# Band attention in fixed rounds, keys a tile ahead, the softmax division on GpSimd

## The chip, the cores and the metric

The kernel runs on one core of a Trainium2 chip. The metric is device time in microseconds (us) of one execution, as the median of several runs. The core has five engines with queues of their own: TensorE (PE in the profile, its weight loads PEld), VectorE (DVE), ScalarE (ACT), GpSimd (POOL) and SyncE (SP), which issues the DMAs here.

## The reference

The reference is one inference step of a one-layer hybrid encoder, width 1024, over 2048 prompt frames and eight running streams of 16 new frames each. One input projection feeds three mixers (band attention, a gated delta rule, a diagonal state-space model); their outputs are concatenated, projected, normed, and pass through a feed-forward block. The change concerns the attention alone: eight heads of width 64, in which a frame sees its own 64-frame chunk and the eight before it, with a learned bias by distance.

```python
s = einsum('bqhd,bkhd->bhqk', qc, kc) * scale + bias
s = where(valid, s, NEG_INF)
p = softmax(s, axis=-1)
return einsum('bhqk,bkhd->bqhd', p, vc)
```

The streams do the same with 512 cached keys and values and their 16 new ones.

## The kernel before

The program has three stages: the projection with the two other mixers, the attention, and then output projection and feed-forward. The change lies in the attention (`attention`, L1071 to L1293).

The prompt is cut into 16 tiles of 128 frames, the heads into four pairs. A tile sees at most five key tiles (its own and four before), fewer in tiles 0 to 3. For each tile and pair:

- `a_scores` multiplies queries by keys. Queries and keys are split into a high part and a rest, stacked on the partitions, so that two matmuls (L1184, L1185) give each segment of scores at full precision; a head has one segment per key block of 512 frames, at most two. VectorE adds the bias and keeps the running extreme (L1186), ScalarE takes the exponential with its sum (L1189), VectorE the reciprocal (L1191) and then the product with it, in place (L1194).
- `a_values` transposes the weights block by block on TensorE (L1212), copies them from PSUM alternately on ScalarE (L1215) and VectorE (L1217), and multiplies by the values (L1220). After the fourth pair the tile's output is copied (L1223) and stored.

`a_kblock` splits the keys of four tiles at once (L1133, L1134), `a_tile` the queries of one (L1155 to L1157). `a_sample` handles one stream whole: its loads, scores (L1269), division (L1274), transposes (L1278, L1282), values (L1289, L1290) and copy (L1293). Streams run in tiles 1 to 8, `w_part` splits a piece of the output projection's weights in tiles 2 to 9.

The values of a pair are written down two pairs behind its scores (`AHEAD` = 2). That order is only the order of writing: the framework's scheduler decides how each engine's instructions are queued, TensorE's too. It allocates a tile's buffer when one of its tag is free, and sets the semaphores.

Of the kernel before, what the change touches and what calls it, by code (L numbers as in the profile page):

```python
# [19 lines left out]
SEQ = 2048  # L20
# [10 lines left out]
AHEAD = 2  # L31
# [13 lines left out]
class K:  # L45
# [1025 lines left out]
    def attention(self, es):  # L1071
# [17 lines left out]
        self.kst, self.vt = {}, {}  # L1089
# [6 lines left out]
        todo = []  # L1096
        for i in range(16):
            t = self.a_tile(i)
            for p in range(4):
                todo.append((t, p, self.a_scores(t, p)))  # L1100
                if len(todo) > AHEAD:
                    self.a_values(*todo.pop(0))
            if 2 <= i <= 9:
                self.w_part(i - 2)
            if 1 <= i <= 8:
                self.a_sample(i - 1)
                if i == 8:
                    nc.sync.dma_start(self.mixT[0:512, SEQ:NT].rearrange("(f p) t -> p f t", p=128), self.sos)

        w0 = c.tile([128, 5, 8, 128], F32, name="w0", tag="nb")  # L1110
        for x in todo:
            self.a_values(*x)
# [4 lines left out]

    def tsplit(self, parts, t):
        src, sl = self.at_a(parts, t)
        return src[:, sl].rearrange("(f p) t -> p f t", p=128)  # L1120

    def a_kblock(self, b):

        nc = self.nc
        ks = self.ak.tile([128, 8, 512], F32R, name="kst", tag="kst")
        for i in range(4):
            kr = self.ak.tile([128, 4, 128], F32, name="kr", tag="kr", bufs=2)
            nc.sync.dma_start(kr, self.tsplit(self.kT, b * 4 + i))
            ts = slice(i * 128, (i + 1) * 128)
            for q in range(2):  # L1130
                r, o = slice(q * 64, q * 64 + 64), slice(64 - q * 64, 128 - q * 64)
                hi = ks[r, q::2, ts]
                nc.scalar.copy(hi, kr[r])  # L1133
                nc.vector.tensor_tensor(ks[o, q::2, ts], kr[r], hi.bitcast(F32), OP.subtract)  # L1134
        self.kst[b] = ks

    def a_tile(self, i):
# [3 lines left out]
        aw = self.aw  # L1141
        b, r = divmod(i, 4)
        if r == 0:
            self.a_kblock(b)
        v = aw.tile([128, 512], F32, name="vt", tag="vt", bufs=6)
        vsrc, sl = self.at_a(self.vS, i)
        nc.sync.dma_start(v, vsrc[sl])
        self.vt[i] = v
        qr = aw.tile([128, 4, 128], F32, name="qr", tag="qr", bufs=2)
        nc.sync.dma_start(qr, self.tsplit(self.qT, i))  # L1150
        qd = aw.tile([128, 8, 128], F32R, name="qd", tag="qd")
# [7 lines left out]
        return dict(i=i, qd=qd, ql=ql, vt=[self.vt[j] for j in range(j0, i + 1)], kst=dict(self.kst), ob=None)  # L1159

    def a_scores(self, t, p):

        nc = self.nc
        V, mm = nc.vector, nc.tensor.matmul
        aw = self.aw
        i, qd, ql, kst = t["i"], t["qd"], t["ql"], t["kst"]
# [6 lines left out]
        for q in range(2):  # L1173
# [4 lines left out]
            if n1:  # L1178
                segs.append((kst[b - 1], min(512 - 128 * n1, 320), 512, 512 - 128 * n1, 0, 128 * n1))
            segs.append((kst[b], 0, max(128 * n2, 192), 0, 128 * n1, 128 * n2))  # L1180
            low = 3e38
            for ks, c0, c1, d0, x0, n in segs:
                ps = self.asp.tile([128, 512], F32, name="aps", tag="s")
                mm(ps[:, c0:c1], qd[:, h], ks[:, h, c0:c1], start=True, stop=False)  # L1184
                mm(ps[:, c0:c1], ql[:, h], ks[:, h, c0:c1], start=False, stop=True)  # L1185
# [11 lines left out]
    def a_values(self, t, p, P):  # L1197
# [28 lines left out]
    def sample_setup(self, es):  # L1226
# [10 lines left out]
        for q in self.sQ:  # L1237
            nc.gpsimd.memset(q, 0.0)
# [547 lines left out]
```

## Time and profile before

| | |
|---|---|
| median of 3 runs | 2952.27 us (2949.34 to 2952.82) |
| the profiled execution's own time | 2949.45 us |
| its span, first to last instruction | 2947.7 us |
| mean granted clock of TensorE | 0.981 of full speed |
| busy: TensorE, VectorE, ScalarE, GpSimd | 2803.6, 1996.0, 1324.7, 930.5 us |

Busy is the time in which an engine had an instruction in it. Matmuls overlap in the array and their ends are modelled, so TensorE's busy time does not say that it ran at its peak. The granted clock is a share of 2.4 GHz; 0.50 is 1.2 GHz.

### The profile page before, as it was taken

Reading aid. Unit: us, or ns where it says so; the run is one execution under the profiler, and the core shown is the slowest. Engines: PE = TensorE matmul, PEld = TensorE weight load, DVE = VectorE, ACT = ScalarE, POOL = GpSimd, SP = SyncE. Lnnn points to the kernel's source line nnn. Section 1 sums busy time; section 2 is a strip of 40 time slices with the busy share of each in tenths; the row PEclk is TensorE's granted clock in tenths of the full one; section 3 lists DMA queues with packets and bytes.
Section 4 is the critical chain, followed back from the end, with each engine's and each line's share of the span. In section 5 each row is a group of like instructions: output and inputs, shape, how many; then the busy total and the mean of one; then the engine's idle time right before and its main releaser. Section 6 shows DMA issues by size and latency. Waiting matters only on the chain.

```text
span 2947.7 us, 46191 instructions
## 1 busy us (share of the span) xinstructions
PE 2803.6 (95%) x16677; PEld 2451.0 (83%) x16677; DVE 1996.0 (68%) x5093; ACT 1324.7 (45%) x2735; POOL 930.5 (32%) x842
## 2 busy tenths in 40 slices
PE   8999999989999999999999999988999998899996
PEld 8988888867777777788889899967999897799996
DVE  7588887797655778778755555497555557855557
ACT  3554544342456666612334344453334345444442
POOL 0011111231100000002554544554544445555653
PEclk9999999989999999999999999999999999999998
DMA  5634454464557441144512122133112122422221
GB/s 183 199 106 127 108 138 112 131 174 122 179 195 224 141 129 51 58 168 165 185 66 86 57 67 77 58 118 122 61 63 81 58 72 95 144 76 73 86 86 43
DMA packets 282923, 330.37 MB, mean 112 GB/s; under 512 B 84530, under 2 KB 217478, under 8 KB 282374
## 3 DMA queue, kind: packets, MB, share of 16 engines
q1 hardware_dynamic: 282694, 327.42, 35.5%
q8 instruction: 131, 2.15, 0.3%
q14 instruction: 98, 0.80, 0.1%
HBM read 265.04 MB, written 64.93 MB: 112 GB/s over the span
## 4 chain that ended last, share of the span: by engine, by line
PE 71%; DVE 15%; DMA 4%; ACT 3%; issue 3%; POOL 3%; SPq 0%; ACTq 0%; POOLq 0%; DVEq 0%
PE fdp L68 7%; PE fdp L69 7%; PE fdp L70 7%; PE pps L69 3%; PE pps L70 3%; PE pps L68 3%; PE aob L1220 2%; PE fupx L69 2%; PE fupx L68 2%; PE fupx L70 2%; PE wops L69 2%; PE wops L68 2%; PE wops L70 2%; PE fupz L70 2%; PE fupz L68 2%
## 5 line engine op out<-in xcount | busy, mean ns | idle before, releaser
L1459 POOL TENSOR_TENSOR wu<-wur,wu 128x512 fp32r<-128x512 f32 x329 | 444.5, 1356 | 683.1 <-ACT wu L1458 672.7
L1585 DVE TENSOR_TENSOR fy<-fy,fdp 128x512 f32<-128x512 f32 x500 | 342.3, 687 | 306.2 <-PE fdp L70 306.0
L68 PE MATMUL fdp<-wdh,hh 128*128 128x512 f32 x1068 | 419.8, 395 | 21.6 <-DVE fy L1583 12.2
L70 PE MATMUL fdp<-wdh,hl 128*128 128x512 f32 x1068 | 418.1, 392 | 1.1 <-DVE hl L1520 1.1
L69 PE MATMUL fdp<-wdl,hh 128*128 128x512 f32 x1068 | 418.7, 392 | 0.0
L1458 ACT CAST wu<-wur 128x512 fp32r<-128x512 f32 x329 | 202.9, 619 | 421.3 <-DMA wur<-in_w_upL 165.1
L68 PE MATMUL pps<-xh,wh 128*128 128x384 f32 (+2 forms) x800 | 280.5, 352 | 9.0 <-ACT xh L63 8.6
L69 PE MATMUL pps<-xl,wh 128*128 128x384 f32 (+2 forms) x800 | 279.5, 350 | 2.9 <-DVE xl L64 2.8
L70 PE MATMUL pps<-xh,wl 128*128 128x384 f32 (+2 forms) x800 | 277.5, 347 | 0.5 <-DVE wl L64 0.3
L68 PEld LDWEIGHTS fdp<-wdh,hh 128*128 128x128 f32 x1068 | 202.2, 190 | 66.0 <-DVE fy L1583 13.8
L70 PEld LDWEIGHTS fdp<-wdh,hl 128*128 128x128 f32 x1068 | 202.1, 189 | 44.3 <-DVE hl L1520 1.9
L69 PEld LDWEIGHTS fdp<-wdl,hh 128*128 128x128 f32 x1068 | 202.1, 189 | 40.2
L63 ACT CAST wdh<-wdr 128x1024 fp32r<-128x1024 f32 x94 | 98.1, 1049 | 262.9 <-PE fdp L70 262.9
L1520 DVE TENSOR_TENSOR hl<-fre,hh 128x384 fp32r<-128x384 f32 (+1 forms) x186 | 137.7, 743 | 71.5 <-ACT hh L1519 71.5
L68 PEld LDWEIGHTS pps<-xh,wh 128*128 128x128 f32 x800 | 152.2, 191 | 19.7 <-ACT xh L63 9.1
L69 PEld LDWEIGHTS pps<-xl,wh 128*128 128x128 f32 x800 | 152.2, 190 | 14.3 <-DVE xl L64 5.4
L70 PEld LDWEIGHTS pps<-xh,wl 128*128 128x128 f32 x800 | 151.9, 190 | 11.3 <-issue 1.8
L64 DVE TENSOR_TENSOR wl<-wr,wh 128x512 fp32r<-128x512 f32 (+1 forms) x152 | 105.3, 699 | 61.1 <-ACT wh L63 57.9
L63 ACT CAST wh<-wr 128x512 fp32r<-128x512 f32 (+1 forms) x152 | 92.8, 619 | 78.2 <-DMA wr<-in_w_inA 39.7
L64 DVE TENSOR_TENSOR wdl<-wdr,wdh 128x1024 fp32r<-128x1024 f32 x94 | 116.1, 1237 | 3.1 <-ACT wdh L63 3.1
L1427 POOL TENSOR_TENSOR fxc<-fxs 128x256 f32<-128x256 f32 x17 | 20.8, 1223 | 294.8 <-ACT fxs L1417 288.8
L1189 ACT ACTIVATE P<-P,st 128x640 f32<-128x640 f32 (+4 forms) x128 | 97.2, 761 | 35.5 <-DVE st L1186 35.3
(555 smaller groups left out, 7289.9 us busy)
## 6 DMA issues: line engine op xcount, KB each, us to landing
wur<-in_w_upL SPq DMA_DIRECT2D x96, 512.0 KB
wdr<-in_w_dnL SPq DMA_DIRECT2D x96, 512.0 KB
wr<-in_w_inA SPq DMA_DIRECT2D x70, 512.0 KB
TU<-tD SPq DMA_DIRECT2D x34, 256.0 KB
y<-in_x SPq DMA_DIRECT2D x17, 512.0 KB
x<-y SPq DMA_DIRECT2D x17, 512.0 KB
fxr<-x SPq DMA_DIRECT2D x17, 512.0 KB
fy<-x SPq DMA_DIRECT2D x17, 512.0 KB
```

What stands on the lines that cost most here:

```text
L63: nc.scalar.copy(hi, src)
L64: nc.vector.tensor_tensor(lo, src, hi.bitcast(F32), OP.subtract)
L68: mm(out, lh, rh, start=first, stop=False, **kw)
L69: mm(out, lh, rl, start=False, stop=False, **kw)
L70: mm(out, ll, rh, start=False, stop=last, **kw)
L1189: nc.scalar.activation(x, x, AF.Exp, scale=-1.0, bias=st[:, q:q + 1], accum_out=st[:, 2 + q:3 + q])
L1220: mm(ob[q * 64:q * 64 + 64, p], vt[j][:, h * 64:(h + 1) * 64], PT[:, k], start=j == 0, stop=j == nk - 1)
L1427: P.tensor_tensor(c1, b["B12"], b["B11"], OP.subtract)
L1458: self.nc.scalar.copy(hi, src)
L1459: P.tensor_tensor(lo, src, hi.bitcast(F32), OP.subtract)
L1520: V.tensor_tensor(hl, r, hh.bitcast(F32), OP.subtract)
L1585: V.tensor_tensor(y[:, zs], y[:, zs], ps, OP.add)
```

## The change

The order of the attention's matmuls on TensorE is written by hand and kept: `mm` and `turn` ask the framework to hold them in program order, from the second round on. A round is one pair of one tile. It issues the scores of its pair, the values of the pair two rounds back, and the transposes of the pair one round back (`a_values` is split into `a_turn` and `a_values`). The product with the reciprocal moves from VectorE to GpSimd (`a_norm`), for the streams too.

The keys are no longer split four tiles at once: `a_load` and `a_keys` load and split those of the next tile during the third round of this one, into two fixed buffers, of which one stretch is filled with zeros at the start. A stream's work is spread over a tile's rounds: scores in the first, transposes in the second, values in the third, and the next stream's K and V are loaded after the scores and the values.

```diff
+        self.kst = [c.tile([128, 8, 512], F32R, name=f"kst{i}") for i in range(2)]
+        for k in self.kst:
+            nc.gpsimd.memset(k[:, :, 128:192].bitcast(F32), 0.0)
...
-        for i in range(16):
-            t = self.a_tile(i)
-            for p in range(4):
-                todo.append((t, p, self.a_scores(t, p)))
-                if len(todo) > AHEAD:
-                    self.a_values(*todo.pop(0))
-            if 2 <= i <= 9:
-                self.w_part(i - 2)
-            if 1 <= i <= 8:
-                self.a_sample(i - 1)
...
+                if streams and p == 0:
+                    sample = self.s_scores(b)
+                    if b < 7:
+                        self.s_load_k(b + 1)
+                if streams and p == 2:
+                    self.s_values(b, sample)
+                    if b < 7:
+                        self.s_load_v(b + 1)
+                rounds.append(self.a_scores(t, p))
+                if len(rounds) > 2:
+                    self.a_values(rounds.pop(0))
+                if len(rounds) > 1:
+                    self.a_turn(rounds[0])
+                self.a_norm(rounds[-1])
+                self.pinned = True
+                if streams and p == 1:
+                    self.s_turn(sample)
+                if i < 15:
+                    if p == 1:
+                        self.a_load(i + 1)
+                    elif p == 2:
+                        self.a_keys(i + 1)
+                    elif p == 3:
+                        t1 = self.a_tile(i + 1)
+                if p == 3 and 2 <= i <= 9:
+                    self.w_part(i - 2)
...
+    def mm(self, *a, **kw):
+
+        i = self.nc.tensor.matmul(*a, **kw)
+        if self.pinned:
+            self.tc.keep_in_program_order(i)
...
+    def a_load(self, i):
+        nc = self.nc
+        kr = self.ak.tile([128, 4, 128], F32, name="kr", tag="kr", bufs=2)
+        nc.sync.dma_start(kr, self.tsplit(self.kT, i))
+        qr = self.aw.tile([128, 4, 128], F32, name="qr", tag="qr", bufs=2)
+        nc.sync.dma_start(qr, self.tsplit(self.qT, i))
+        self.ld_[i] = kr, qr
+
+    def a_keys(self, i):
+
+        nc = self.nc
+        kr, ks = self.ld_[i][0], self.kst[i // 4 % 2]
+        ts = slice(i % 4 * 128, i % 4 * 128 + 128)
+        for q in range(2):
+            r, o = slice(q * 64, q * 64 + 64), slice(64 - q * 64, 128 - q * 64)
+            hi = ks[r, q::2, ts]
+            nc.scalar.copy(hi, kr[r])
+            nc.vector.tensor_tensor(ks[o, q::2, ts], kr[r], hi.bitcast(F32), OP.subtract)
+        v = self.aw.tile([128, 512], F32, name="vt", tag="vt", bufs=6)
         vsrc, sl = self.at_a(self.vS, i)
         nc.sync.dma_start(v, vsrc[sl])
         self.vt[i] = v
...
-        rs = aw.tile([128, 2], F32, name="rs", tag="ars", bufs=4)
-        V.reciprocal(rs, st[:, 2:4])
+        return dict(t=t, p=p, P=P, st=st, nk=nk)
+
+    def a_norm(self, s):
+        P, st = s["P"], s["st"]
+        rs = self.aw.tile([128, 2], F32, name="rs", tag="ars", bufs=4)
+        self.nc.vector.reciprocal(rs, st[:, 2:4])
         for q in range(2):
-            x = P[:, q, 0:128 * nk]
-            V.tensor_scalar(x, x, rs[:, q:q + 1], None, OP.mult)
-        return P
...
+            x = P[:, q, 0:128 * s["nk"]]
+            self.nc.gpsimd.tensor_scalar(x, x, rs[:, q:q + 1], None, OP.mult)
...
-        V.tensor_scalar(P, P, st[:, 2:3], None, OP.mult)
-        PT = self.aw.tile([128, 10, 128], F32, name="sPT", tag="PT")
+        nc.gpsimd.tensor_scalar(P, P, st[:, 2:3], None, OP.mult)
+        return dict(P=P)
```

## Rows read from the trace of the kernel before

**Rows 1.** Windows: length; busy (instructions) of PE, PEld, DVE, ACT, POOL; clock; DMA; GB/s.
```profile
925.70:1139.50 213.80, 202.36 (x1676) 159.64 (x1675) 157.58 (x504) 133.41 (x298) 7.09 (x24) 0.93 0.42 129
1139.50:1246.00 106.50, 99.04 (x890) 76.94 (x890) 92.49 (x283) 78.99 (x172) 0.00 (x0) 1.00 0.16 47
```

**Rows 2.** Line L1223: duration ns min/median/max, first and last start us.
```profile
L1223 ACT COPY aos<-aob x16: 563/586/589, 925.7 to 1246.0; 128x512 f32<-128x512 f32 x16
```

**Rows 3.** Timeline of ScalarE near 1139: start us, duration us, [idle before <-releaser].
```profile
1139.47 0.59 ACT L1223 COPY aos<-aob 128x512 f32<-128x512 f32 x1 [1.26 <-PE aob L1220]
```

**Rows 4.** Timeline of TensorE, 900 to 920.
```profile
914.44 0.25 PE L1184 MATMUL aps<-kst,qd 128*128 128x192 f32 x1
```

**Rows 5.** Timeline of TensorE, 1209 to 1214.
```profile
1209.85 1.25 PE L1212 MATMUL tps<-ld_c_ident,P 128*128 128x128 f32 x10
1210.86 0.36 PE L1184 MATMUL aps<-kst,qd 128*128 128x256 f32 x1
1211.06 0.28 PE L1185 MATMUL aps<-kst,qlz 128*128 128x256 f32 x1
1211.18 0.34 PE L1184 MATMUL aps<-kst,qd 128*128 128x384 f32 x1
1211.36 0.33 PE L1185 MATMUL aps<-kst,qlz 128*128 128x384 f32 x1
...
1211.86 1.31 PE L1220 MATMUL aob<-PT,vt 128*64 128x128 f32 x20
1213.10 0.44 PE L1184 MATMUL aps<-kst,qd 128*128 128x384 f32 x1
```

**Rows 6.** Timeline of TensorE, 978 to 992, a stream's values.
```profile
982.08 1.06 PE L1289 MATMUL aob<-sPT,sV 128*128 128x32 f32 x8
...
983.20 1.20 PE L1289 MATMUL aob<-sPT,sV 128*128 128x32 f32 x8
```

**Rows 7.** Windows of 2 us over the end of those values.
```profile
984.00:986.00 2.00, 2.00 (x12) 2.00 (x11) 0.00 (x0) 0.00 (x0) 0.00 (x0) 0.50 0.01 4
```

**Rows 8.** Groups by form, 913 to 1246: busy us, mean ns, idle before, releasers.
```profile
L1189 ACT ACTIVATE P<-P,st 128x640 f32<-128x640 f32 x96 | 79.4, 828 | 34.3 <-DVE st L1186 34.2
...
L1194 DVE TENSOR_SCALAR P<-P,rs 128x640 f32<-128x640 f32 x96 | 48.7, 548 | 0.5
...
L1215 ACT COPY PT<-tps 128x512 f32<-128x512 f32 x60 | 34.8, 579 | 38.0 <-PE tps L1212 27.8 <-PE aob L1220 3.5 <-PE aob L1290 3.0
...
L1189 ACT ACTIVATION_READ_ACCUMULATOR P<-P,st 128x1 f32 x128 | 24.2, 189 | 0.0
...
L1157 DVE TENSOR_TENSOR qlz<-qr,qd 64x512 fp32r<-64x512 f32 x28 | 19.1, 684 | 0.5
...
L1134 DVE TENSOR_TENSOR kst<-kr,kst 64x512 fp32r<-64x512 f32 x16 | 11.0, 686 | 0.5
...
L1133 ACT CAST kst<-kr 64x512 fp32r<-64x512 f32 x16 | 9.8, 614 | 1.5 <-DMA kr<-kT 1.3
```

**Rows 9.** Windows of line L1194 alone: stretch, length, VectorE's busy us.
```profile
925.70:1139.50 213.80, 34.74 (x74) 0.93 0.42 129
1139.50:1246.00 106.50, 22.27 (x44) 1.00 0.16 47
```

**Rows 10.** Groups by form of GpSimd over the whole span.
```profile
L1464 POOL TENSOR_TENSOR wur<-wur 128x512 f32<-128x512 f32 x48 | 63.0, 1312 | 3.8
...
L729 POOL MEMSET Sb<- 128x1024 f32 x4 | 3.8, 952 | 2.4 <-PE bqs L650 2.4
...
L1235 POOL TENSOR_SCALAR nbs<-rvs 128x528 f32<-128x528 f32 x1 | 1.5, 1536 | 11.1 <-PE aps L1184 11.1
```

**Rows 11.** Window of line L1186 alone, VectorE's busy us.
```profile
913.00:1246.00 333.00, 111.14 (x448) 0.95 0.35 107
```

**Rows 12.** Waits of SP's queue, 800 to 1246: us in total, times, longest.
```profile
SPq L1147 <- PE aob L1220: 100.3, 10, 16.0
```

**Rows 13.** Tile fxc on GpSimd: duration ns min/median/max, first and last start.
```profile
L1427 POOL TENSOR_TENSOR fxc<-fxs x17: 732/843/2685, 1312.5 to 2472.7; 128x256 f32<-128x256 f32 x17
```

More of the change, by code (lines that the diff above doesn't have):

```diff
@@ L30 @@
 NDIAG = 4
-AHEAD = 2
 PACE1 = 2
@@ L1116, in attention, with turn @@
         self.w_tile(0, self.y0, h, l, lambda: self.asp.tile([128, 512], F32, name="aps", tag="s"))
+    def mm(self, *a, **kw):
+        i = self.nc.tensor.matmul(*a, **kw)
+        if self.pinned:
+            self.tc.keep_in_program_order(i)
+    def turn(self, out, src):
+        i = self.nc.tensor.transpose(out, src, self.ident)
+        if self.pinned:
+            self.tc.keep_in_program_order(i)
     def tsplit(self, parts, t):
@@ L1120, in tsplit @@
         return src[:, sl].rearrange("(f p) t -> p f t", p=128)
-    def a_kblock(self, b):
+    def a_load(self, i):
         nc = self.nc
[L1125 to L1135, printed above, removed]
+        kr = self.ak.tile([128, 4, 128], F32, name="kr", tag="kr", bufs=2)
[13 more added lines that the diff above has]
+        v = self.aw.tile([128, 512], F32, name="vt", tag="vt", bufs=6)
+        vsrc, sl = self.at_a(self.vS, i)
+        nc.sync.dma_start(v, vsrc[sl])
+        self.vt[i] = v
     def a_tile(self, i):
@@ L1140, in a_tile @@
         V = nc.vector
[L1141 to L1151, printed above, removed]
+        qr = self.ld_[i][1]
+        qd = self.aw.tile([128, 8, 128], F32R, name="qd", tag="qd")
         ql = self.qlz[i % 2]
@@ L1158, in a_tile @@
         j0 = max(0, i - 4)
-        return dict(i=i, qd=qd, ql=ql, vt=[self.vt[j] for j in range(j0, i + 1)], kst=dict(self.kst), ob=None)
+        return dict(i=i, qd=qd, ql=ql, vt=[self.vt[j] for j in range(j0, i + 1)], ob=None)
     def a_scores(self, t, p):
         nc = self.nc
-        V, mm = nc.vector, nc.tensor.matmul
+        V = nc.vector
         aw = self.aw
-        i, qd, ql, kst = t["i"], t["qd"], t["ql"], t["kst"]
+        i, qd, ql = t["i"], t["qd"], t["ql"]
         b, r = divmod(i, 4)
@@ L1216, in a_values @@
             else:
-                V.tensor_copy(PT[:, u:u + len(m)], src)
-        for k, (q, j) in enumerate(units):
+                nc.vector.tensor_copy(PT[:, u:u + len(m)], src)
+    def a_values(self, s):
+        nc = self.nc
+        t, p, PT, nk = (s[k] for k in ("t", "p", "PT", "nk"))
+        i, vt = t["i"], t["vt"]
+        if t["ob"] is None:
+            t["ob"] = self.aop.tile([128, 4, 128], F32, name="aob", tag="o")
+        ob = t["ob"]
+        for k, (q, j) in enumerate(s["units"]):
             h = 2 * p + q
-            mm(ob[q * 64:q * 64 + 64, p], vt[j][:, h * 64:(h + 1) * 64], PT[:, k], start=j == 0, stop=j == nk - 1)
+            self.mm(ob[q * 64:q * 64 + 64, p], vt[j][:, h * 64:(h + 1) * 64], PT[:, k], start=j == 0, stop=j == nk - 1)
         if p == 3:
-            os_ = aw.tile([128, 4, 128], F32, name="aos", tag="qr", bufs=2)
+            os_ = self.aw.tile([128, 4, 128], F32, name="aos", tag="qr", bufs=2)
             nc.scalar.copy(os_, ob)
@@ L1235, in sample_setup @@
         nc.gpsimd.tensor_scalar(nb, rv[:, ::-1], -1.0, None, OP.mult)
-        self.sQ = [c.tile([128, 4, 32], F32, name=f"sQ{i}") for i in range(1)]
-        for q in self.sQ:
-            nc.gpsimd.memset(q, 0.0)
+        self.sQ = c.tile([128, 4, 32], F32, name="sQ")
+        nc.gpsimd.memset(self.sQ, 0.0)
         self.sos = c.tile([128, 4, 128], F32, name="sos")
```

93 lines of the change are left out of this document (55 added, 38 removed).

## The prediction

> **What bounds the kernel now.** I read the windows by stage first [rows 1], because the page's TensorE share of the whole span is an average over stages with other limits. The change touches only the attention stage, which ends with the last output copy at 1246.0 us; the first such copy is at 925.7 [rows 2]. I cut it at 1139.5, when the tenth of these sixteen copies starts [rows 3]: *stream part* (tiles 1 to 9, 213.8 us, with the eight sample streams and the loads of w_out) and *late part* (tiles 10 to 15, 106.5 us). TensorE's first score matmul is at 914.4, right behind the last of the projection's [rows 4], so nothing ahead of that can be won.
>
> A busy TensorE is not a full one, so I take its real work from distances between starts [rows 5]: ten transposes take 1.0 us (1209.85 to 1210.86), twenty value instructions 1.24 (1211.86 to 1213.10), a 256-column score matmul 0.12, a 384-column one 0.175. A round of one pair of heads over five key tiles is then eight score matmuls (1.2), ten transposes (1.0) and twenty value instructions (1.25): 3.45 us. The late part has 24 rounds of values: 83 us of 106.5. VectorE is busy 92.5 there, 87%, and ScalarE 79.0, 74% [rows 1]: the late part is VectorE's.
>
> In the stream part TensorE needs 312 units (a unit is one transposed block with its two value instructions: 0.225), 70 us; scores by the same distances, fewer columns in the early tiles, 37; and eight streams at about 6.2 (scores 1.2 by estimate, five transposes 0.5, and values of 4 x 1.13, the distance between blocks of ten [rows 6]), 50. That is 157 at full clock. The granted clock is 0.93 there: of its two levels, 1.2 and 2.4 GHz, the lower holds 14% of the 213.8 us, which costs 15. The drop comes during the narrow value matmuls of a stream, which keep TensorE busy throughout: it is 0.50 from 984 on, in the block that begins in the rows above [rows 7]. So the need is 172, 80%. VectorE stands at 157.6 (74%), ScalarE at 133.4 (62%). This part is TensorE's, with about 42 us in which it waits or starts late.
>
> **The change, part by part.** *Division.* VectorE loses 128 multiplications, 548 ns each at 128x640 [rows 8], of which 34.7 us lie in the stream part and 22.3 in the late one [rows 9], and the eight of the streams. VectorE falls to 70.2 in the late part.
>
> GpSimd's price X for a 128x640 multiplication by a column is not in the trace. Below: a fill, which reads nothing, takes 952 ns for 1024 elements, so 0.60 us. Above: the one tensor-by-scalar instruction, on 528 elements read backwards, took 1.54 us, which scales to 1.86; two-input operations take 1.31 for 512 [rows 10], and scale to 1.64. One input should cost less than two, and the 1.54 is the first and only one of its kind; I take 1.15. GpSimd then works 2.3 us in a round, under any round's length below.
>
> *The chain.* In the fixed order a round issues scores of r, values of r-2, transposes of r-1. From the start of scores r: 0.55 until VectorE can start (two matmuls 0.175 apart, the second 0.34 long [rows 5]); four reductions at 0.5 (111.14 us for 224 with their read-outs [rows 11]), 2.0; the last exponential 0.83 and its sum 0.19 [rows 8]; reciprocal and four hand-overs, by my estimate 0.55; then 2X: 4.1 + 2X. Transposes of r come at the end of the following round, so two rounds hold this chain and one block of transposes: round = (4.1 + 2X + 1.0)/2 = 2.55 + X. That is 3.2, 3.7 or 4.4 us for X of 0.60, 1.15 or 1.86.
>
> *Late part.* Per round: TensorE 3.45, chain 3.7, VectorE 70.2/22 = 3.2, ScalarE 79.0/22 = 3.6 (22 rounds of scores fall in it). The limits lie close together. VectorE, the bound now, reaches 87%; granting the same to ScalarE gives 3.6/0.87 = 4.15, above the chain. Now it is 106.5/24 = 4.44. Gain 24 x 0.29 = 7.
>
> *Fixed order on TensorE and spread sample work.* Scores, transposes and values of a stream are set into three different rounds, its K and V loaded a tile ahead. VectorE keeps at most 158 - 35 - 4 = 119 in the stream part; the keys come back onto it. Now only 16 of the 32 key splits run after 913 [rows 8], the rest lie under the projection; with keys one tile ahead up to 14 more move in: 14 x 0.69 on VectorE and 14 x 0.61 on ScalarE, giving 129 and 142. Both stay below TensorE's 172, which covers them; without that cover they would cost up to 10. With TensorE the clear bound and its order no longer waiting for VectorE's multiplications, I grant it the same 87%: 172/0.87 = 198, gain 16. At 95% it would be 181, gain 33; at 80%, as now, nothing.
>
> *Queues.* Per tile the same DMAs are issued. Today the value load waits in SP's queue for TensorE's old values 100.3 us in all [rows 12], with everything issued behind it; in the change it stands after the round that frees its buffer, so SP's queue can only shorten. Key and query loads lead their split by one round, about 4 us; a late one would hold ScalarE, which now waits 1.3 us in all for key loads [rows 8]. I cost the queue, the two fills of the key tiles (about 0.5 each by the fill of [rows 10], under the projection) and the added key dependence at tiles 0, 4, 8, 12 at nothing; that last would cost 1 us each if the split were late.
>
> *End.* The last round has no other to hide GpSimd: 2X - 1.0 = 1.3 lost. Sum: -16 - 7 + 1.3 = -22 against the profiled execution's own 2949.45 (span 2947.7): 2927.5 us. That execution lies 2.8 under the median of 2952.27, within the runs shown.
>
> **A rule against it.** VectorE and GpSimd do get in each other's way here: a GpSimd subtraction of 128x256 has a median of 843 ns and a longest of 2685 [rows 13], though other causes of that length are not excluded. The Trainium skill, SBUF — State Buffer, section "Who interferes with whom", says that a VectorE instruction with two SBUF inputs and a GpSimd instruction that reads SBUF exclude each other for the whole instruction. This case's longest duration fits it without proving it. By the usual durations of the rows the sum stays 2927.5; with every such meeting paid in full it would be the second rival's 2950.
>
> **The rivals.** *A queue turns the chain into a circle (slower).* If a PSUM copy of round r stands on ScalarE ahead of an exponential of round r+1, that exponential waits for GpSimd. The circle is 0.65 until the first copy can start (four transposes and the tail of the last), copy 0.58, exponential 1.02, reciprocal and hand-overs 0.45, and 2X: 2.7 + 2X per round. At X = 1.15 it is 5.0, at 1.86 it is 6.4. It decides from X = 0.87, where it passes the 4.44 of now. For it: ScalarE would be nearly full, and it now idles 27.8 us before these copies, waiting for transposes [rows 8]. Against it: scores of r+1 are issued before transposes of r, so its exponential is ready first. Late part +13 at X = 1.15, stream part gaining 0 to 8, end +1.3: 2956; at 1.86 the late part gives +47, 2998; I take 1.3 (5.3), +21, 2966 with a stream gain of 6.
>
> *Exclusion eats it (no change).* VectorE keeps about 75 two-input subtractions (28 query and 30 key splits at 0.68 [rows 8], 16 weight splits). If each waited a whole X, the late part's 18 would add 21, bringing VectorE back to 91 of 106.5, and the stream part's 57 would add 66, VectorE 195, above TensorE's 172. Then nothing is won: about 2950. With GpSimd busy 55% of a round and half an instruction left on average, it is 75 x 0.55 x 0.57 = 24, on an engine with room; so it gets a small chance.
>
> *The change does more.* If TensorE's waits go (stream part at 95%, -33) and ScalarE packs to 95% in the late part (3.8 a round, -15), the time is 2903.
>
> **How the numbers follow.** Anything under 0.2% (5.9 us) is about what a measurement of this kernel can't tell from no change. Forecast 0.55, circle on ScalarE 0.21, exclusion 0.14, more 0.10. The forecast's own range is 2906 (33 + 12 gained) to 2950 (X = 1.86, chain 4.4 plus 0.2: late part +4, stream gain 6, end +2.7). Over all cases 2903 to 2960 leaves out the circle at high X and gains beyond the third rival, under 2 in 10. Faster takes the forecast but for its upper end (0.51), the third rival (0.10) and a little of the second (0.01): 0.62; slower 0.22, the circle and a bad end of the second; same 0.16.
>
> **What would show it.** Right: the multiplication on GpSimd at 0.9 to 1.4 us; VectorE under 75 us in the late part's rounds and ScalarE its fullest engine; rounds of about 4.15 without a stream; the stream part under 205 us; the clock still falling behind stream values only. Wrong: transposes waiting for GpSimd in most rounds (circle, or X near its upper end), key and query subtractions of over 1 us (exclusion), a granted clock at 0.50 in the late part, or score matmuls waiting for key or query splits at tile changes.

## The result, and the profile after

The kernel after takes 3048.86 us (median of 4 runs, 3047.74 to 3051.81), the kernel before in the same job 2950.81: a ratio of 1.0334, interval 1.0316 to 1.0352. The prediction, 2927.5 with a range to 2960 and 0.22 for slower, was wrong. The profiled execution took 3047.74, its span 3045.7.

The windows from the first to the tenth and on to the sixteenth output copy of the kernel after (columns as in [rows 1]):

```profile
938.40:1215.90 277.50, 231.98 (x1667) 192.77 (x1668) 131.81 (x424) 140.53 (x303) 143.23 (x104) 0.79 0.33 100
1215.90:1344.00 128.10, 100.89 (x891) 83.57 (x891) 74.88 (x240) 79.81 (x170) 87.22 (x46) 0.93 0.13 38
```

Beside [rows 1] the stream part is 63.7 us longer and the late part 21.6. VectorE was relieved as foreseen (92.5 to 74.9 in the late part), and no engine is near full in either part. TensorE's clock fell from 0.93 to 0.79 and from 1.00 to 0.93. From the first score (918.2 here, 914.4 in [rows 4]) to the first output copy it took 20.2 us for 11.3. That makes 94.3 us; the other 3.8 lie ahead of the first score, in the projection, where the later kernels' first scores scatter from 908.6 to 916.5. That scatter is part of every difference between two whole times below; the sums of the three stretches are free of it.

GpSimd's groups by form over the attention of the kernel after (busy us, mean ns, idle before and its releasers):

```profile
L1242 POOL TENSOR_SCALAR P<-P,rs 128x640 f32<-128x640 f32 x96 | 183.4, 1924 | 119.9 <-DVE rs L1239 104.6 <-PE aps L1154 13.4 <-PE tps L1159 1.4
L1242 POOL TENSOR_SCALAR P<-P,rs 128x512 f32<-128x512 f32 x8 | 12.9, 1632 | 12.2 <-DVE rs L1239 12.1
...
L1242 POOL TENSOR_SCALAR P<-P,rs 128x128 f32<-128x128 f32 x8 | 4.7, 604 | 16.3 <-DVE rs L1239 16.3
...
L1284 POOL TENSOR_SCALAR nbs<-rvs 128x528 f32<-128x528 f32 x1 | 1.8, 1751 | 0.0
```

The product costs 1.92 us on average, not 1.15, and more than the 1.86 taken as its upper bound. Its usual length is 1.88 (the median); ten of the 96 took 2.10 to 2.69, and each of these ten started while VectorE was in a subtraction of two inputs. 512 elements at 1.63 are dearer than the two-input subtraction of 512 in [rows 10] (1.31). What followed can be read from the waits over the same stretch (us in total, times, longest):

```profile
POOL P L1242 <- DVE rs L1239: 159.2, 37, 13.6
ACT P L1233 <- DVE st L1230: 89.0, 48, 9.9
DVE PT L1258 <- PE tps L1159: 88.6, 46, 4.9
PE tps L1159 <- POOL P L1242: 68.9, 64, 2.7
```

The attention has 64 rounds, and its transposes waited 64 times for GpSimd, 68.9 us, and GpSimd 159.2 us for the next reciprocals: engines that take turns, none of them full. The timeline of the late part shows it (start us, duration, idle before and its releaser):

```profile
1259.28 1.31 PE L1159 MATMUL tps<-ld_c_ident,P 128*128 128x128 f32 x10
...
1260.41 0.69 DVE L1258 COPY PT<-tps 128x512 f32<-128x512 f32 x1 [1.22 <-PE tps L1159]
...
1261.06 0.17 DVE L1239 RECIPROCAL rs<-st 128x2 f32<-128x2 f32 x1
...
1261.39 4.10 POOL L1242 TENSOR_SCALAR P<-P,rs 128x640 f32<-128x640 f32 x2 [3.79 <-PE aps L1154]
...
1265.54 1.20 PE L1159 MATMUL tps<-ld_c_ident,P 128*128 128x128 f32 x9 [1.89 <-POOL P L1242]
...
1266.56 0.69 DVE L1258 COPY PT<-tps 128x512 f32<-128x512 f32 x1 [0.91 <-PE tps L1159]
```

Transposes at 1259.3, a PSUM copy of theirs on VectorE at 1260.4, behind that copy the next round's reciprocal, then two products, then the next transposes at 1265.5: 6.3 us for a round, and 3.79 us in which GpSimd had nothing to do.

### The profile page after: what moved, and what is told of

Read it like the earlier page. It is cut to its first block, busy times and chain, and to the rows that moved or that the text cites. A ratio compares the mean times of both kernels' runs of the same rounds, so it can differ in the third digit from the quotient of the medians.

```text
span 3045.7 us, 46334 instructions
## 1 busy us (share of the span) xinstructions
PE 2837.8 (93%) x16677; PEld 2490.7 (82%) x16677; DVE 1947.0 (64%) x4957; ACT 1329.5 (44%) x2735; POOL 1162.0 (38%) x980
## 4 chain that ended last, share of the span: by engine, by line
PE 51%; DVE 7%; POOL 7%; issue 2%; ACT 1%; DMA 1%; SPq 0%; POOLq 0%; ACTq 0%; DVEq 0%
PE fdp L67 7%; PE fdp L68 7%; PE fdp L69 7%; POOL P L1242 5%; PE aob L1154 2%; PE tps L1159 2%; PE fupx L67 2%; PE fupx L68 2%; PE fupx L69 2%; PE wops L67 2%; PE wops L68 2%; PE wops L69 2%; PE fupz L69 2%; PE fupz L67 2%; PE fupv L69 2%
## 5 line engine op out<-in xcount | busy, mean ns | idle before, releaser
L1242 POOL TENSOR_SCALAR P<-P,rs 128x640 f32<-128x640 f32 (+4 forms) x128 | 218.8, 1723 | 176.1 <-DVE rs L1239 159.2
L68 PEld LDWEIGHTS fdp<-wdl,hh 128*128 128x128 f32 x1068 | 202.0, 189 | 40.0
L68 PEld LDWEIGHTS pps<-xl,wh 128*128 128x128 f32 x800 | 152.8, 191 | 14.2 <-DVE xl L63 5.1
L1159 PE MATMUL tps<-ld_c_ident,P 128*128 128x128 f32 x560 | 95.4, 310 | 69.0 <-POOL P L1242 68.9
L1159 PEld LDWEIGHTS tps<-ld_c_ident,P 128*128 128x128 f32 x560 | 69.5, 154 | 91.1 <-POOL P L1242 83.7
```

The lines of the kernel that those rows point to most:

```text
L68: mm(out, lh, rl, start=False, stop=False, **kw)
L1159: i = self.nc.tensor.transpose(out, src, self.ident)
L1242: self.nc.gpsimd.tensor_scalar(x, x, rs[:, q:q + 1], None, OP.mult)
```

## The experiments

The table gives each kernel's time, its ratio to the kernel before in its own job, and from its profile the stretches that the text compares: first score to first output copy (start), first to tenth copy (stream part) and tenth to sixteenth (late part), with the clock of the last two.

| kernel | us | ratio (interval) | start | stream part, clock | late part, clock |
|---|---|---|---|---|---|
| before | 2952.27 | | 11.3 | 213.8, 0.93 | 106.5, 1.00 |
| after | 3048.86 | 1.0334 (1.0316 to 1.0352) | 20.2 | 277.5, 0.79 | 128.1, 0.93 |
| 1 after, division on VectorE | 2964.37 | 1.0043 (1.0028 to 1.0059) | 16.7 | 230.4, 0.84 | 102.2, 1.00 |
| 2 before, division on GpSimd | 2978.02 | 1.0083 (1.0058 to 1.0107) | 13.3 | 235.0, 0.86 | 110.8, 1.00 |
| 3 after, order free | 3011.75 | 1.0198 (1.0173 to 1.0222) | 13.2 | 248.9, 0.84 | 133.3, 0.92 |
| 4 after, reciprocal first | 3041.33 | 1.0296 (1.0270 to 1.0321) | 19.7 | 272.5, 0.80 | 136.0, 0.90 |
| 5 after, all queues written in order | 3037.17 | 1.0286 (1.0268 to 1.0304) | 17.2 | 279.2, 0.77 | 125.1, 0.95 |
| 6 after, one head on each | 2987.90 | 1.0118 (1.0099 to 1.0137) | 17.9 | 242.5, 0.83 | 111.7, 1.00 |
| 7 as 1, stream values wide | 2939.56 | 0.9958 (0.9941 to 0.9974) | 15.8 | 200.5, 1.00 | 102.3, 1.00 |
| 8 as 1, stream values between scores | 2973.38 | 1.0073 (1.0057 to 1.0090) | 16.8 | 237.8, 0.81 | 102.3, 1.00 |
| 9 after, one round later | 2962.92 | 1.0033 (1.0020 to 1.0045) | 20.3 | 229.2, 0.83 | 95.7, 1.00 |
| 10 as 9, wide | 2931.60 | 0.9929 (0.9910 to 0.9948) | 20.9 | 202.0, 0.98 | 95.0, 1.00 |
| 11 before, wide | 2929.59 | 0.9922 (0.9905 to 0.9938) | 10.0 | 195.2, 1.00 | 106.6, 1.00 |
| 12 as 7, one round later | 2929.23 | 0.9924 (0.9906 to 0.9942) | 17.9 | 191.8, 1.00 | 99.2, 1.00 |
| 13 after, wide | 3022.08 | 1.0229 (1.0206 to 1.0252) | 20.2 | 253.3, 0.89 | 128.3, 0.93 |
| 14 as 10, one head on each | 2938.64 | 0.9948 (0.9929 to 0.9966) | 19.6 | 198.5, 0.98 | 103.6, 1.00 |

**1 and 2: the division alone, in either kernel.**

```diff
-            self.nc.gpsimd.tensor_scalar(x, x, rs[:, q:q + 1], None, OP.mult)
+            self.nc.vector.tensor_scalar(x, x, rs[:, q:q + 1], None, OP.mult)
```

The streams' product goes with it; the second experiment is the opposite edit of the kernel before.

> The changed kernel with the division put back on VectorE, for the prompt and the streams; the fixed order, the spread streams and the keys a tile ahead stay. Theory (GpSimd's price, 1.92 us for 128x640, held in a circle: product, transposes, VectorE's PSUM copy, reciprocal of the next round, product): the circle shrinks by 2 x (1.92 - 0.55) = 2.7 us a round, no transposes wait for the product, the attention ends before 1260 us and the whole takes 2925 to 2965 us. Rival 1 (the fixed order on TensorE is what costs, whoever divides): still above 3000. Rival 2 (a narrow stream block now drops the clock for longer): late part (tiles 10 to 15) as fast as before, stream part still 40 us or more slower, about 2995.

> The kernel before with its division alone moved to GpSimd, for the prompt and the streams; its order is the scheduler's. Theory (price in a circle): the circle exists here too wherever a PSUM copy stands ahead of a reciprocal in VectorE's queue, but TensorE can take other rounds' scores while it waits, so a part of the loss: 2975 to 3030 us. Rival 1 (the fixed order costs): as before or faster, 2930 to 2955, since VectorE loses 60 us of work.

Without GpSimd the kernel after is 84 us faster, 76.5 of it in the attention (425.8 and 349.3, the sums of the table's three stretches); its late part is 4.3 shorter than before. So GpSimd's division makes most of the loss. In the kernel before it costs only 25; the third experiment bears on why. Both times came out as expected (2925 to 2965, 2975 to 3030), the first near its upper end. What the first experiment leaves is a stream part that is 16.6 us longer than before, at a clock of 0.84.

**3 and 4: the fixed order, and one queue.** The third takes the order off (`self.pinned = True` left out). The fourth writes reciprocal and products right behind their scores and keeps the reciprocal ahead of the PSUM copies on VectorE:

```diff
                 rounds.append(self.a_scores(t, p))
+                self.a_norm(rounds[-1])
...
+        i = self.nc.vector.reciprocal(rs, st[:, 2:4])
+        if self.pinned:
+            self.tc.keep_in_program_order(i)
```

The two `keep_in_program_order` lines stand at the VectorE copy too.

> The changed kernel without the fixed order on TensorE (nothing is held in program order), GpSimd dividing. Theory (price in a circle): most of the loss stays, 3010 to 3050 us. Rival 1 (the fixed order costs): the loss is gone, at most 2965.

> The changed kernel, GpSimd dividing, with the reciprocals and VectorE's PSUM copies held in an order in which the reciprocal of a round stands ahead of the copy of the round before. The work is the same. Theory (price in a circle through VectorE's queue): the circle is open, a round is bound by the prediction's chain over two rounds, (4.1 + 2 x 1.92 + 1.0)/2 = 4.5 us, against 5.3 of the changed kernel's late part; late part 105 to 115 us instead of 128, the whole 2970 to 3010. If the price alone counts (GpSimd's own chain, with no circle), it stays within 10 us of 3049.

With GpSimd dividing, the fixed order costs 28.6 us in the stream part and 7.0 at the start, and saves 5.2 in the late part: 30.4 in the attention. Of the 37 us between the whole times, the rest is scatter (first score at 918.2 and 910.0). Most of the loss stays without the fixed order, as the theory had it.

So it isn't the scheduler's freedom that makes GpSimd's division cheap in the kernel before. That kernel differs in another way: `a_values` holds the transposes too, so they are written two pairs behind their scores (`AHEAD` = 2), and the change writes them one round behind. The traces follow the writing. Counted from the matmuls' starts, from tile 2 on, the scores of 2.0 later rounds on average have started when a round's transposes start in the kernel before, 2.1 in the second experiment, 1.2 in the third with its order free, 1.0 in the kernel after. TensorE's waits for GpSimd ahead of the prompt's transposes go with that distance (us in total, times, longest; second experiment, then third):

```profile
PE tps L1212 <- POOL P L1194: 5.3, 9, 1.2
PE tps L1158 <- POOL P L1241: 60.5, 57, 1.9
```

In the second a stream's transposes wait 15.9 us more for their own product.

The copy ahead of the reciprocal, which the timeline above seems to accuse, is not the cause alone. In the kernel after, 40 of the 64 reciprocals started more than 0.25 us after the last sum that they need, 66.9 us in all, 34 of them with a PSUM copy of VectorE in between. In the fourth there are 23, 30.5 us in all, none behind a copy, but 16 behind a reduction of the next scores, which took the copy's place in the queue. The attention did not gain by it: its stretches sum to 428.2 us for 425.8, the late part grew, and the 7.5 us by which the whole is shorter lie ahead of the first score (910.7 for 918.2). The theory's 105 to 115 us for the late part failed; the other description, within 10 us of 3049, held.

**5: every member of the circle.** Reductions, reciprocals and copies on VectorE, exponentials and copies on ScalarE are all to be kept in program order, `a_norm` written early as in the fourth:

```diff
+    def keep(self, i):
+        if self.pinned:
+            self.tc.keep_in_program_order(i)
...
-            nc.scalar.activation(x, x, AF.Exp, scale=-1.0, bias=st[:, q:q + 1], accum_out=st[:, 2 + q:3 + q])
+            self.keep(nc.scalar.activation(x, x, AF.Exp, scale=-1.0, bias=st[:, q:q + 1], accum_out=st[:, 2 + q:3 + q]))
```

> The kernel after, with the reductions, reciprocals and PSUM copies of VectorE and the exponentials, PSUM copies and output copies of ScalarE held in program order too, the reciprocal and its two products written right behind the scores. No instruction that waits for GpSimd can then stand ahead of one that GpSimd waits for. Theory (the loss is a circle of queue members, whichever they are): a round takes two-round chain over two, (4.1 + 2 x 1.92 + 1.0)/2 = 4.5 us, the late part some 24 x 4.5 = 108 to 114 us (128.1 in the kernel after), the time 2965 to 3000. Rival (GpSimd's product is too long for two rounds whatever the order, or VectorE and GpSimd hinder each other): late part over 122, time 3025 to 3060.

The late part is 125.1, 3 us less than after and on the rival's side. The timeline of the late part shows a first reason:

```profile
1264.62 0.17 DVE L1243 RECIPROCAL rs<-st 128x2 f32<-128x2 f32 x1 [0.99 <-ACT P L1237]
...
1264.95 3.75 POOL L1246 TENSOR_SCALAR P<-P,rs 128x640 f32<-128x640 f32 x2 [1.17 <-PE tps L1163]
...
1268.76 1.20 PE L1163 MATMUL tps<-ld_c_ident,P 128*128 128x128 f32 x9 [1.04 <-POOL P L1246]
...
1268.85 0.17 DVE L1243 RECIPROCAL rs<-st 128x2 f32<-128x2 f32 x1 [0.99 <-ACT P L1237]
...
1269.18 3.75 POOL L1246 TENSOR_SCALAR P<-P,rs 128x640 f32<-128x640 f32 x2 [0.48 <-DVE rs L1243]
...
1272.99 1.20 PE L1163 MATMUL tps<-ld_c_ident,P 128*128 128x128 f32 x9 [0.35 <-POOL P L1246]
```

In this stretch the queues are in the order written, a round takes 4.2 us, and the transposes still wait for GpSimd: the chain of scores, reductions, exponentials, reciprocal, products and transposes is as long as the two rounds it is given.

But the circle was not open everywhere. In 14 of the 64 rounds, six of them in the late part, a reduction of the next round's scores still stands in VectorE's queue ahead of the reciprocal, although it is written behind it. Here two do: a round of this tile has 384 columns first, one of the next tile has 256 first.

```profile
1287.01 0.42 DVE L1234 CUSTOM_DVE_ANT_0 P<-aps,nb 128x256 f32<-128x256 f32 x1 [4.04 <-PE aps L1154]
...
1287.59 0.62 DVE L1234 CUSTOM_DVE_ANT_0 P<-aps,nb,st 128x384 f32<-128x384 f32 x1
...
1288.13 0.16 DVE L1243 RECIPROCAL rs<-st 128x2 f32<-128x2 f32 x1
...
1288.46 7.47 POOL L1246 TENSOR_SCALAR P<-P,rs 128x640 f32<-128x640 f32 x4 [4.26 <-DVE rs L1243]
```

VectorE waits 4.04 us for the next scores, GpSimd 4.26 for the reciprocal behind them. Together these reciprocals start 29.4 us after the last sum that they need, 14.2 of it in the late part. So this run doesn't refute the circle; why the order was not kept is not known. Nor is the circle all: two late tiles without such a reciprocal took 21.3 and 19.3 us, 5.3 and 4.8 a round, where the theory had 4.5. The last tile, which has no key or query to split for a next one, takes 18.1 us, 4.5 a round; the five before it take 21.4 on average. The difference, 3.3, is about the four subtractions that a tile has on VectorE (means of 0.75 us in the kernel after, 3.0), and about those reciprocals too (14.2 over five tiles, 2.8). Which of the two makes it is not shown.

**6: half the product.** One head on GpSimd, the other on VectorE (`e = self.nc.gpsimd if q == 0 else self.nc.vector`).

> The kernel after, with the product of a pair's first head on GpSimd and of its second on VectorE. The product's part in the chain falls from 3.84 to 1.92 us a round. Theory of the circle (about 6.3 us where it closes, 3.84 of it the product): nearly all of the late part's loss goes, 104 to 110 us, and the stream part comes to 235 to 250; time 2965 to 2990. Rival (every GpSimd product costs the same by contention with VectorE's reads): half of the 84 us between the kernel after and the one with the division on VectorE, 3005 to 3010.

It gave back 61 of the 84 us, 53.7 of 76.5 in the attention: more than half, so the chain's length counts, and not a fixed price for each product. Time and stream part lie in the theory's ranges, the late part (111.7) just above.

**9: more distance.** The same instructions on the same engines, but transposes two rounds and values three behind their scores, the stream's values a round later:

```diff
-                if len(rounds) > 2:
+                if len(rounds) > 3:
                     self.a_values(rounds.pop(0))
-                if len(rounds) > 1:
+                if len(rounds) > 2:
                     self.a_turn(rounds[0])
```

> The kernel after with transposes two rounds and values three rounds behind their scores (there one and two), and the stream's values in the fourth round. Same instructions, same engines. The chain from scores to transposes then has three rounds: (4.1 + 2 x 1.88 + 1.0)/3 = 3.0 us a round, under GpSimd's own 3.77 and under the other engines. Theory (GpSimd's product is too long for the distance, not for the engine): the late part, where no stream disturbs, comes to 24 x 4.15 to 4.4 = 100 to 106 us (128.1 in the kernel after), the whole to 2960 to 2985, with the clock after the streams still low. Rival (GpSimd is itself the bound or hinders the others): late part over 118, whole over 3020.

This decides the late part, which has no streams. With GpSimd as slow as ever (median 1.884), and no queue in order but TensorE's, it fell from 128.1 to 95.7, below before and below what either theory expected:

```profile
933.00:1162.20 229.20, 210.99 (x1666) 180.26 (x1667) 131.63 (x432) 137.43 (x304) 141.09 (x104) 0.83 0.39 119
1162.20:1257.90 95.70, 88.70 (x884) 74.91 (x884) 70.41 (x229) 72.52 (x164) 84.57 (x46) 1.00 0.17 49
```

TensorE's waits for GpSimd ahead of the prompt's transposes, 68.9 us in 64 times in the kernel after, are all but gone, and GpSimd's last 16 products follow each other without a pause:

```profile
PE tps L1160 <- POOL P L1243: 1.5, 2, 1.2
```

```profile
1222.72 29.80 POOL L1243 TENSOR_SCALAR P<-P,rs 128x640 f32<-128x640 f32 x16 [0.54 <-DVE rs L1240]
```

GpSimd is busy 84.6 of 95.7 us and TensorE 88.7; the third and second tile from the end take 15.1 and 15.2, that is 3.8 a round, twice GpSimd's 1.88. Its delay no longer sets the pace. That its throughput now does is not shown: none of TensorE's waits for it lies in the late part, and the twelfth has late tiles of 15.0 and 15.5 with GpSimd idle. The edit gives the circle through VectorE's queue more time as well, so it doesn't tell the chain's own length from what queues add to it. The whole is 86 us faster than after, 80.6 of it in the attention.

**7 and 8: the clock behind the streams.** Seventh, on top of the first, a stream's values move all 128 columns of the transposed weights where 32 are wanted; the rest is thrown away:

```diff
-            out, hs, qs = ob[:, p, 0:32], slice(p * 128, p * 128 + 128), slice(p * 32, p * 32 + 32)
+            out, hs, qs = ob[:, p], slice(p * 128, p * 128 + 128), slice(0, 128)
```

with the final copies picking the 32. The eighth keeps the 32 and sets the four blocks of values one by one between the score matmuls.

> Division on VectorE as in the first experiment (2964 us, its stream part 230.4 at a clock of 0.84); beyond it the values of a stream move all 128 columns of the transposed weights where 32 are wanted, four times the columns in 160 matmuls, the rest thrown away. Theory (the narrow values of a stream pull the clock to 0.50 for 6 us behind them): clock of the stream part 0.92 or more, stream part 205 to 220, time 2940 to 2955, although there is more work. Rival (the 17 us come from the waits around the stream's pieces, the clock only follows the waits): stream part 231 to 240, time 2965 to 2975.

> Division on VectorE as in the first experiment; the four blocks of a stream's values are set one by one between the score matmuls of the third round, where they stood as one block ahead of them. Same work, same narrow columns. Theory of the clock: no long stretch of narrow matmuls is left, clock of the stream part 0.92 or more, 205 to 222 us, time 2940 to 2956. Rival (waits around the pieces): 228 to 238, time within 5 us of 2964, or worse since the scores now wait for the stream's PSUM buffer.

The first experiment's windows of 3 us over a stream's narrow values, from 1030.3 to about 1035.8, and behind them (columns as in [rows 1]):

```profile
1030.00:1033.00 3.00, 2.71 (x25) 2.71 (x25) 1.12 (x3) 2.70 (x5) 0.00 (x0) 1.00 0.08 24
1033.00:1036.00 3.00, 3.00 (x19) 3.00 (x19) 0.00 (x0) 1.14 (x2) 0.00 (x0) 0.61 0.00 0
1036.00:1039.00 3.00, 3.00 (x16) 2.78 (x18) 2.57 (x8) 0.34 (x1) 0.00 (x0) 0.50 0.70 177
```

and the seventh's over the same work, values from 1020.0 to 1024.5:

```profile
1021.00:1024.00 3.00, 3.00 (x30) 3.00 (x29) 0.69 (x1) 0.82 (x2) 0.00 (x0) 1.00 0.00 0
1024.00:1027.00 3.00, 3.00 (x35) 2.75 (x33) 2.20 (x13) 0.00 (x0) 0.00 (x0) 1.00 0.38 77
```

TensorE is busy nearly all through both. In the last of the four blocks of narrow values the clock falls to 0.50 (1.2 GHz), and the scores and values behind it run at half speed; with the wide ones it stays at 1.00 (2.4 GHz). At full clock the wide ones cost no more time. Since the ends of matmuls are modelled, the distance between the starts of two blocks of ten tells it, first experiment and then seventh (start, duration):

```profile
1031.43 1.06 PE L1154 MATMUL aob<-sPT,sV 128*128 128x32 f32 x8
...
1032.54 1.06 PE L1154 MATMUL aob<-sPT,sV 128*128 128x32 f32 x8
```

```profile
1021.20 1.06 PE L1154 MATMUL aob<-sPT,sV 128*128 128x128 f32 x8
...
1022.32 1.06 PE L1154 MATMUL aob<-sPT,sV 128*128 128x128 f32 x8
```

That is 1.11 and 1.12 us. The records of all streams' matmuls with the weights sV agree (duration ns min/median/max):

```profile
L1154 PE MATMUL aob<-sPT,sV x256: 276/297/403, 929.0 to 1122.0; 128*128 128x32 f32 x128
```

```profile
L1154 PE MATMUL aob<-sPT,sV x256: 275/275/378, 933.9 to 1097.8; 128*128 128x128 f32 x128
```

Four times the columns, and the minimum is the same. Stream part 230.4 to 200.5, time 2964 to 2940, below the kernel before and just below the theory's ranges. The eighth fell on the rival's side, worse than the first: narrow values between wide score matmuls held the clock at 0.50 for longer (0.50 in the windows from 1036 to 1042, TensorE busy throughout). So my picture of one long block that must be broken up was wrong; what helped was the number of columns. Why fewer columns at the same spacing lower the clock, no run shows.

**10 to 13: which cause is worth what.** The tenth joins the ninth and the seventh's edit, the eleventh is the kernel before with that edit alone, the twelfth has wide values, division on VectorE and the longer distance, the thirteenth is the kernel after with wide values alone.

> The kernel before this one in the list, and the stream's values over all 128 columns as well. If both theories hold (distance for GpSimd, narrow columns for the clock), clock 1.00 from the second tile on, stream part 192 to 205, late part 100 to 106, time 2935 to 2950, about that of the wide kernel with the division on VectorE (2939.6), or a few us less because VectorE has room. If GpSimd is a bound of its own: over 2990.

> The kernel before, with only the stream's values over all 128 columns. In the kernel before the clock of the stream part is 0.93 and that part takes 213.8 us. Theory of the clock: the clock rises to about 1.00, the part to 198 to 208, the time to 2936 to 2948, so that the fixed order and the keys a tile ahead are worth 0 to 5 us beside it. Rival (the low clock of the kernel before has another cause, waits between tiles): no change, 2950 to 2960, a little slower for the added columns.

> Wide stream values and division on VectorE (2939.6 us) with transposes two and values three rounds behind their scores. With the product at 0.55 us on VectorE two rounds are enough ((4.1 + 1.1 + 1.0)/2 = 3.1), so distance gives nothing: late part 100 to 103 (102.3 without it), time within 5 us of 2939.6. Rival (distance itself relieves TensorE, whoever divides): late part under 98.

> The kernel after, with only the stream's values over all 128 columns. The width alone took 27 us from the stream part at the longer distance (229.2 to 202.0) and 30 with the division on VectorE. If the causes add up: stream part 247 to 255 (277.5 in the kernel after), late part unchanged at 125 to 130, time 3015 to 3025. If the waits for GpSimd lower the clock by themselves: stream part 262 or more at a clock under 0.90, time over 3030.

The tenth's, eleventh's and twelfth's windows, stream part and then late part of each (tenth first):

```profile
932.20:1134.20 202.00, 178.79 (x1666) 150.40 (x1667) 133.49 (x477) 137.33 (x305) 142.04 (x101) 0.98 0.45 135
1134.20:1229.20 95.00, 88.64 (x884) 74.92 (x883) 69.43 (x229) 72.51 (x163) 84.72 (x46) 1.00 0.17 49
```

```profile
921.60:1116.80 195.20, 184.51 (x1672) 147.55 (x1671) 162.94 (x554) 133.93 (x298) 5.35 (x24) 1.00 0.47 144
1116.80:1223.40 106.60, 99.02 (x893) 76.84 (x893) 92.40 (x281) 78.30 (x172) 0.00 (x0) 1.00 0.16 46
```

```profile
930.50:1122.30 191.80, 174.96 (x1656) 146.69 (x1657) 162.80 (x553) 136.27 (x301) 5.99 (x21) 1.00 0.47 142
1122.30:1221.50 99.20, 91.04 (x891) 75.46 (x891) 89.52 (x278) 74.58 (x166) 0.00 (x0) 1.00 0.17 49
```

With the four combinations of distance and width on GpSimd, the stream part divides cleanly: 277.5 (near, narrow), 229.2 (far, narrow), 253.3 (near, wide), 202.0 (far, wide). Distance is worth 48 to 51 us, width 24 to 27, and they add. The thirteenth met the first description in all its numbers, and of the second only the clock, 0.89. So the clock is low there for a further reason. The waits for GpSimd go with it: the late part, which has no streams, has 0.93 in the kernel after and 1.00 with the same instructions at the longer distance.

The eleventh is the plainest result: one edit of the old kernel, in a part that the change did not mean to touch, gives 0.8%, as much as everything else together (twelfth, 2929.23). It came out 6 us below what I had expected, the tenth 3. The clock of the eleventh is 1.00 in both parts, and the late part is as before. The twelfth's distance was expected to give nothing and gave 10 us against the seventh, 3 of them in the late part and 9 in the stream part, 2 lost at the start; why VectorE's product gains from it was not looked into.

**14: both engines.** The tenth with one head's product on each.

> Transposes two rounds behind, wide stream values, and the product of a pair's first head on GpSimd, of its second on VectorE. Busy a round in the late part: GpSimd 1.88, VectorE about 3.4, ScalarE 3.1, TensorE 3.7. If TensorE is what is left (88.6 us busy of 95.0 with all products on GpSimd): late part 92 to 97, stream part 188 to 200, time 2922 to 2932, no more than 0.3% from either pure form. If GpSimd's length still held the stream part (202.0 against 191.7): stream part 190 to 194 and the time 2920 to 2926.

Neither forecast held, though the stream part (198.5) is in the first's range: the late part is 103.6, longer than with either engine alone (95.0 and 99.2). Line L1244 of that kernel, the product on either engine (duration ns min/median/max):

```profile
L1244 DVE TENSOR_SCALAR P<-P,rs x64: 286/667/1109, 916.2 to 1226.5; 128x640 f32<-128x640 f32 x48, 128x128 f32<-128x128 f32 x4, 128x256 f32<-128x256 f32 x4, 128x384 f32<-128x384 f32 x4
L1244 POOL TENSOR_SCALAR P<-P,rs x64: 607/1886/2249, 916.4 to 1226.7; 128x640 f32<-128x640 f32 x48, 128x128 f32<-128x128 f32 x4, 128x256 f32<-128x256 f32 x4, 128x384 f32<-128x384 f32 x4
```

Started together by one reciprocal, the two lengthen each other: VectorE's, at most 0.58 us for all 128 of the twelfth, takes up to 1.11. Over 24 rounds that is some 5 us on VectorE (0.78 on average at 640 against 0.55), not all of the 8.6 and not shown to lie on the path.

## Why the prediction was wrong

*X, the price of the product.* The sum took 1.15, because "one input should cost less than two" and the only row of the kind read backwards. Both reasons failed: one input with a column costs more than two, and the backward instruction was no exception; its row scaled, 1.86, was the answer (median 1.883, minimum 1.879). This is the first step that failed, a term 0.7 too small, twice in a round. It isn't the largest: at X = 1.86 the prediction's own working gives 2950, 22.5 of the 121 us that are missing. The others lie mostly in the stream part, 63.7 us longer where 16 less were forecast, and come from the chain and the clock. The Trainium skill, GPSIMD Engine Reference, section "Engine selection", calls one-input work on GpSimd "roughly line-rate" beside VectorE; the trace differs, 1.88 us against VectorE's 0.548 [rows 8], and the measurement decides.

*The chain.* Its formula, 2.55 + X, came near: 4.4 at X = 1.88, and 4.5 in the last tile. What failed is how it was used, "above the chain": as one limit beside the engines' busy times, the largest to count. It is as long as its two rounds, so whatever else stands ahead of its members in an engine's queue is added to it. The late part took 5.3 a round while every engine had room, 21.8 us more than 24 rounds of 4.43. The 13 late reciprocals there come to 21.8 too; the equal numbers don't prove that they are all of it, and the splits of the next tile are a second candidate. In the stream part, where the prediction saw TensorE "no longer waiting for VectorE's multiplications", TensorE's transposes waited 37.9 us for GpSimd's; distance alone is worth 48 to 51 there.

*The distance.* The prediction counted the two rounds of the new order and didn't compare them with the old one, whose transposes stand two pairs behind their scores. So the change lengthened the chain by GpSimd's product and took a round of its distance away. That with the round given back the late part is 95.7 (ninth), and that the division cost 25 us where the distance was kept (second), shows it.

*The circle.* The rival had the right sign and the right engine, and at X = 1.86 gave 2998, still 51 too low. Its place was wrong: on ScalarE the last exponential of a round started more than 0.35 us late in eight rounds, 7.5 us in all, and the copies that stood in the way stood on VectorE, ahead of the reciprocal. How much this circle adds to the chain stays open, since neither the fourth nor the fifth run opened it fully. The range, which left out the circle at high X, ended 89 us too low.

*The late part.* VectorE falls to 74.9, just below the 75 that was named, over a longer stretch than foreseen; in the ninth it is the 70.4 of the working (70.2). The 99 us that I expected lie between what the change gives with VectorE dividing (102.2) and with GpSimd and more distance (95.7). So a gain was there, and the distance lost it. With VectorE dividing, it doesn't come from relief: VectorE is busy 92.0 us, as before.

*The stream part.* "TensorE the clear bound ... 172/0.87" took TensorE's 172 as work that stays. It isn't: at wide values the fixed order takes 191.8 to 202.0 at a clock of 0.98 to 1.00 (seventh, tenth, twelfth), at narrow ones 229 and 230 at 0.83 and 0.84 (ninth, first). The clock was read, and its 15 us were put into the need as a cost that stays. For the kernel before, that size was near (213.8 to 195.2, 18.6 with wide values); in the first experiment it is 30. So the fixed order made the low clock longer, for which the sum had no term; why it does is not shown. With the clock set right, the fixed order at the old distance gains nothing on the eleventh (200.5 against 195.2), at the longer one 3.4 (191.8), where 16 were forecast.

*The start.* The sum had no term for the stretch from the first score to the first output copy. It grew by 8.9, of which 5.4 are there with VectorE dividing too.

*Exclusion.* VectorE's key and query subtractions rose from 0.69 and 0.68 to 0.75 and 0.76 on average, 53 of them: 4 us. Six took over 1 us, the rival's sign, the longest 1.20. The rival at full price is refuted. The Trainium skill, SBUF — State Buffer, section "Who interferes with whom", has one engine block the other for its whole instruction; here those subtractions grew by at most 0.51 us beside products of 1.88 (0.64 in the ninth), and products started together (fourteenth) cost VectorE at most 0.56. The ten long products of the kernel after, each started inside a subtraction, fit its sense but grew by 0.2 to 0.8 us. No run here separates which of its conditions applied.

*Queues.* "SP's queue can only shorten" was wrong: the value load waited 109.1 us for [rows 12]'s 100.3, a stream's value and key loads 64.1 and 44.5 us for TensorE, where those of the kernel before have 31.2 and 34.6. It cost little, since ScalarE's key splits waited 0.4 us in all for their loads.

## What to carry to other kernels

A chain that crosses engines must be compared with the distance that the order gives it, before it is compared with busy times: an engine at 68% of a stage can hold all others if its delay doesn't fit, and one more round of distance can be worth more than any relief. Before a new order is written, count the distance that the old one has. When the price of an operation is open, take the row of the same kind, however odd its form, and look where the sign flips between the bounds. A low granted clock in a stretch is a cost like any other; find the instructions ahead of its fall, and try what it takes to change them, even with more work.

## What the runs showed that was not expected

Blocks of ten matmuls over 32 and over 128 columns with 128x128 weights start 1.11 and 1.12 us apart at full clock, and with the first kind the clock falls to 0.50 with TensorE busy, with the second it stays at 1.00. A product by a column on GpSimd takes 604 ns for 128 elements a partition and 1883 (median) for 640, some 2.5 ns for each further one. In the kernel after it was longer only where it started inside a VectorE subtraction of two inputs, up to 2694; in the fourteenth, up to 2249 where VectorE's own product started with it. Three quite different kernels, with VectorE busy 69 to 92 us of the late part and GpSimd idle or nearly full there, end within 2.4 us of each other (2929.23, 2929.59, 2931.60).
